# Sums of second-product weights by accumulating transfers instead of VectorE, in a Winograd feed-forward of one transformer layer

## The chip, the cores and the metric

The kernel runs on one core of a Trainium2 chip. The metric is the device time of one execution in microseconds (us); a kernel's time is the median of its runs. Engines are named as in the profile: PE is TensorE (matmul), PEld its weight load, DVE is VectorE, ACT is ScalarE, POOL is GpSimd, SP is SyncE, whose queue starts most transfers.

## The reference

One layer of a diffusion transformer over 1024 tokens of width 1024, with 256 context tokens: a half-step SwiGLU feed-forward, token mixing (a grid Fourier transform beside a bidirectional chunkwise mLSTM), a second half-step feed-forward. All in f32. What the change touches is the second product of the two feed-forwards of the 1024 tokens, `(silu(a) * b) @ w2`, with w2 of 2816 x 1024:

```python
def swiglu(u, w13, w2):
    a, b = jnp.split(u @ w13, 2, axis=-1)
    return (jax.nn.silu(a) * b) @ w2

def half_ffn(h, shift, scale, gate, g_pre, g_post, w13, w2):
    u = modulate(rmsnorm(h, g_pre), shift, scale)
    return h + 0.5 * gate * rmsnorm(swiglu(u, w13, w2), g_post)
```

The adaLN values (shift, scale, gate) are products of a conditioning vector with `w_ada`, nine chunks of 1024.

## The kernel before, in words

Every matmul runs in three passes on operands split into a high and a low part (`mm3`: hi·hi, hi·lo, lo·hi). A split is a cast on ACT and a subtraction on VectorE: L145 and L146 in `split_act`, L140 and L141 in `wunit`.

The feed-forwards use a Winograd scheme: the product of 2 x 2 blocks in seven products instead of eight, for sums of the left blocks a and of the right blocks b. `ffn_in` forms the left operands and writes the seven of them to a DRAM scratch `gx` (`put`, L479; the sums are made in `sink`, with `add` and `sub` of L582 and L583). `wino_out`, called once for each feed-forward, does the seven products with w2, one after another in the order 1, 6, 7, 4, 5, 3, 2. The blocks of w2 are b11, b12 (upper rows, left and right half of the columns) and b21, b22. The right operands are b11 for product 1; T2 = b22 − b12 + b11 for 6; T3 = b22 − b12 for 7; b21 − T2 for 4; b12 − b11 for 5; b22 for 3; b21 for 2. Each product has 11 pieces k of 128 rows, taken in six steps of two (the last has one); a piece takes 12 matmuls of 128x512, a product some 30 us.

For each step, `weights(n, s)` makes the right operand and splits it to `wh` and `wl` (three buffers each), and `operand` (L774) loads a left operand X from `gx` to a tile `t` and splits it to two tiles `g`. Weights come in two ways, both by SP: `raw` (L733) loads 512 KB, two pieces, to a tile `wr` (three buffers); `held` (L738) loads 256 KB to a tile `g`, of which there are 36, shared with the split X. T2 and T3 stay in `g` from product 1 or 6 to product 4 or 7. The sums of weights are `tt`, L727, on VectorE:

```python
            elif n == 6:
                b12 = raw(0, s, 1)
                for c, k in zip(cs, s):
                    T3[k] = held(1, k, 1)
                    tt(T3[k], T3[k], b12[:, c], SUB)
                    tt(T2[k], T3[k], T2[k], ADD)
```

Beside the products runs background work, issued in portions between matmuls (`tick`): in the first run of `wino_out` the remaining adaLN chunks (`ada_rest`: loads of `w_ada` at L247, sums at L253 on VectorE, small matmuls L263) and the preparation of the context; in the second the transposition of the residual stream to tokens (`to_tokens`: load `u<-h` L1556, transposes L1560, stores to `h2t` L1563). A scheduler orders the instructions of every engine ahead of time; the queue of each engine is in order, and tiles come from pools whose buffers are reused when their readers are done. `post` (L293 on) makes the gains with which a block's output is scaled.

Of the kernel before, what the change touches and what calls it, by code (L numbers as in the profile page):

```python
# [13 lines left out]
ALU = mybir.AluOpType  # L14
# [3 lines left out]
ND = D // P  # L18
SEQ = 1024
CTX = 256  # L20
TB = 512
# [13 lines left out]
class Kernel:  # L35
# [259 lines left out]
    def post(self, s, i):  # L295

        nc = self.nc
        t = self.const([P, ND], f"post{s}{i}")
        nc.vector.scalar_tensor_tensor(
            t, self.ada[s][:, (3 * i + 2) * 8 : (3 * i + 3) * 8], 1.0 if i == 1 else 0.5,  # L300
            self.norm_g[:, (2 * i + 1) * 8 : (2 * i + 2) * 8], op0=ALU.mult, op1=ALU.mult)
        return t


# [127 lines left out]
    NP = NF // 2  # L432
# [101 lines left out]
    def pair_products(self, q, n0, W, U, gx, gates):  # L534


        nc = self.nc
        p, h = q // 2, q % 2

        def product(n, acc=None):  # L540
            wh, wl = W[n]
            new = acc is None
            if new:
                acc = self.mm()
            for k in range(4):
                self.tick(1 / 8)
                c = slice(k * P, (k + 1) * P)
                self.mm3(acc, (wh[:, c], wl[:, c]), (U[n][0][k], U[n][1][k]), new and k == 0, k == 3, not new)
            return acc

        made = {}

        def sink(t, j, b):
            if h == 0:
                gates[j, b] = self.s512("m")
                nc.scalar.activation(gates[j, b], t, AF.Silu)
                return
            made[j, b] = self.gated(t, gates.pop((j, b)))
            if (j, b) != (0, 1):
                self.put(p, made[j, b], gx, {(0, 0): 1, (1, 0): 2, (1, 1): 4}[j, b])  # L560
            else:

                a11, a21, a22 = made[0, 0], made[0, 1], made[1, 1]
                s1, s2 = self.s512("t"), self.s512("t")
                add(s1, a21, a22)
                self.put(p, s1, gx, 5)
                sub(s2, s1, a11)
                self.put(p, s2, gx, 6)
                sub(a21, a11, a21)
                self.put(p, a21, gx, 7)  # L570
                made["s2"] = s2
            if (j, b) == (1, 0):
                s4 = self.s512("t")
                sub(s4, made[1, 0], made["s2"])
                self.put(p, s4, gx, 3)

        def copy(src):
            t = self.s512("t")
            nc.scalar.copy(t, src)
            return t  # L580

        add = lambda o, x, y: nc.vector.tensor_tensor(o, x, y, op=ALU.add)  # L582
        sub = lambda o, x, y: nc.vector.tensor_tensor(o, x, y, op=ALU.subtract)  # L583
        if p >= n0:
            A = product(1)
            p1 = copy(A)
            yield 1
            E = product(2)
            add(p1, E, p1)
            sink(p1, 0, 0)  # L590
            yield 2
            product(6, A)
            u2 = copy(A)
            yield 6
            Dp = product(7)
            p7 = copy(Dp)
            yield 7
            product(5, A)
            y = copy(A)
            add(p7, p7, y)  # L600
            sink(p7, 1, 1)
            yield 5
            product(4, Dp)
            add(u2, Dp, u2)
            sink(u2, 0, 1)
            yield 4
            product(3, A)
            sink(A, 1, 0)
            yield 3
            return  # L610
        p1 = W["p1"]
        if h == 1:
            made[0, 0] = self.s512("t")
            nc.sync.dma_start(made[0, 0], gx[0, p * P : (p + 1) * P, :])
        u2 = self.s512("t")
        add(u2, product(6), p1)
        yield 6
        Dp = product(7)
        p7 = copy(Dp)
        add(p7, p7, u2)  # L620
        yield 7
        C = product(5)
        add(p7, C, p7)
        sink(p7, 1, 1)
        yield 5
        product(4, Dp)
        t = self.s512("t")
        add(t, Dp, u2)
        sink(t, 0, 1)
        yield 4  # L630
        product(3, C)
        add(u2, C, u2)
        sink(u2, 1, 0)
        yield 3
# [81 lines left out]

    def wino_out(self, w2, gx, tokens, done):


        nc = self.nc
        w = w2.rearrange("(p j c) o -> c j p o", j=2, c=P)
        NP = self.NP
        steps = [tuple(range(k, min(k + 2, NP))) for k in range(0, NP, 2)]
        T2, T3 = [None] * NP, [None] * NP
        tt = lambda o, x, y, op: nc.vector.tensor_tensor(o, x, y, op=op)  # L727
        ADD, SUB = ALU.add, ALU.subtract

        def raw(j, s, h):  # L730
            t = self.sb.tile([P, 1024], F32, tag="wr", bufs=3, name=self.name("wr"))
            v = t.rearrange("p (a b) -> p a b", a=2)
            nc.sync.dma_start(v[:, : len(s), :], w[:, j, s[0] : s[-1] + 1, h * TB : (h + 1) * TB])  # L733
            return t

        def held(j, k, h):
            t = self.s512("g")
            nc.sync.dma_start(t, w[:, j, k, h * TB : (h + 1) * TB])  # L738
            return t

        def weights(n, s):
            hi = self.sb.tile([P, 1024], F32R, tag="wh", bufs=3, name=self.name("wh"))
            lo = self.sb.tile([P, 1024], F32R, tag="wl", bufs=3, name=self.name("wl"))
            cs = [slice(i * TB, (i + 1) * TB) for i in range(len(s))]
            full = slice(0, len(s) * TB)
            one = None
            if n == 1:
                for k in s:
                    T2[k] = held(0, k, 0)
            elif n == 6:  # L750
                b12 = raw(0, s, 1)
                for c, k in zip(cs, s):
                    T3[k] = held(1, k, 1)
                    tt(T3[k], T3[k], b12[:, c], SUB)
                    tt(T2[k], T3[k], T2[k], ADD)
            elif n == 4:
                one = raw(1, s, 0)
                for c, k in zip(cs, s):
                    tt(one[:, c], one[:, c], T2[k], SUB)
            elif n == 5:  # L760
                one, b11 = raw(0, s, 1), raw(0, s, 0)
                tt(one[:, full], one[:, full], b11[:, full], SUB)
            elif n in (2, 3):
                one = raw(1, s, n - 2)
            if one is not None:
                self.split_act(hi[:, full], lo[:, full], one[:, full])
            else:
                for c, k in zip(cs, s):
                    self.split_act(hi[:, c], lo[:, c], (T3 if n == 7 else T2)[k])
            return [(hi[:, c], lo[:, c]) for c in cs]  # L770

        def operand(n, k):
# [12 lines left out]
        for n in (1, 6, 7, 4, 5, 3, 2):  # L785
# [4 lines left out]
            for s in steps:  # L790
                T = weights(n, s)
                X = [operand(n, k) for k in s]
                todo += [(k, x, t) for k, x, t in zip(s, X, T)]
                if n == 2 and s[-1] in steps[-2]:
                    continue
                order = [(i, d) for i in range(len(todo)) for d in range(4)]
                if n == 2 and len(todo) > 2:
                    order = [(i, d) for d in range(4) for i in range(len(todo))]
                for i, d in order:
                    k, x, t = todo[i]  # L800
                    self.tick(1 / 8)
                    c = slice(d * P, (d + 1) * P)
                    st, mv = (x, t) if tokens else (t, x)
                    self.mm3(acc[d], (st[0][:, c], st[1][:, c]), mv, new and k == 0, k == NP - 1, not new)
                    if n == 2 and k == NP - 1:
                        done(0, 0, d, kept[1][d], acc[d])
                todo = []
# [1002 lines left out]
```

## Time and profile before

| | us |
|---|---|
| median of 3 runs (2751.29 to 2759.47) | 2755.34 |
| profiled execution | 2761.97 |
| its span | 2760.1 |
| product 1, 6, 7, 4, 5 of the first run: from | 490, 524, 565, 599, 632 (5 ends at 672) |
| product 1, 6, 7, 4, 5 of the second run: from | 2516, 2558, 2594, 2624, 2656 (5 ends at 2688) |

The profile shows one execution. The granted TensorE clock over all of it was 0.986 of full speed. The starts of the products are read from the order of TensorE's matmuls on a time line. Rows of groups read: line, engine, operation, out<-in by the program's names, sizes, how many, then busy us in sum, mean ns of one, then the engine's idle time just before them and what ended most of it.

### The profile page before, as it was taken

To read this page: it belongs to the slowest core of one execution; us is meant where nothing else is said; L and a number is where in the kernel's file an instruction comes from. 1 tells how busy PE (TensorE), PEld (TensorE's weight loads), DVE (VectorE), ACT (ScalarE), POOL (GpSimd) and SP (SyncE) were. 2 spreads that over 40 slices of the span, in tenths; PEclk is the share of its full clock that TensorE was granted. 3 is DMA by queue.
4 is the path that set the end of the run, shared out by engine and by line. 5 is a ranking of instruction groups with operands and counts; after the bars stand their busy time and mean duration, and the time that the engine had idled before them with its cause. 6 is when DMAs were issued, how large, how long until landed. Compare 5 with 4: busy or idle time off the path is not lost.

```text
span 2760.1 us, 33923 instructions
## 1 busy us (share of the span) xinstructions
PE 2661.3 (96%) x11657; PEld 2114.7 (77%) x11657; DVE 1857.2 (67%) x3341; ACT 1106.8 (40%) x1893; POOL 100.6 (4%) x217
## 2 busy tenths in 40 slices
PE   8899999998999999999999999999999999998998
PEld 5688888776877777777777778778887788887776
DVE  5688887899786438565363674555667887863765
ACT  4543332444454337233333333433345433333552
POOL 1100000000000001000000000000001000000000
PEclk9999999999999999999999999999999999999999
DMA  9765454857686545325223452356556654536874
GB/s 300 242 206 164 155 167 133 309 190 252 210 252 211 170 134 173 102 69 155 79 77 103 133 142 77 94 150 196 181 157 210 183 169 153 168 107 198 293 247 139
DMA packets 426012, 472.51 MB, mean 171 GB/s; under 512 B 25497, under 2 KB 264642, under 8 KB 425840
## 3 DMA queue, kind: packets, MB, share of 16 engines
q1 hardware_dynamic: 424448, 468.53, 54.2%
q0 software_dynamic: 1248, 1.75, 0.2%
q8 instruction: 92, 1.51, 0.2%
q14 instruction: 80, 0.66, 0.1%
q10 hardware_dynamic: 144, 0.07, 0.0%
HBM read 373.21 MB, written 97.04 MB: 170 GB/s over the span
## 4 chain that ended last, share of the span: by engine, by line
PE 75%; DVE 9%; DMA 8%; issue 4%; ACT 2%; SPq 1%; POOL 0%; DVEq 0%; POOLq 0%; ACTq 0%
PE mm L153 67%; DMA m<-r_l 2%; PE aux L1147 2%; PE qc L1332 1%; DVE u L253 1%; DVE wl L141 1%; DVE g L146 1%; DMA ld<-in_w_ada_dram 1%; DMA ld<-h 1%; DMA u<-h 1%; DMA ld<-hn 1%; PE mm L234 1%; DMA t<-gx 0%; ACT wh L140 0%; DVE wl L146 0%
## 5 line engine op out<-in xcount | busy, mean ns | idle before, releaser
L153 PE MATMUL mm<-g,wh 128*128 128x512 f32 (+1 forms) x2552 | 839.6, 409 | 11.9 <-ACT g L145 5.0
L153 PEld LDWEIGHTS mm<-g,wh 128*128 128x128 f32 (+1 forms) x2552 | 484.2, 192 | 122.2 <-ACT wh L145 6.0
L153 PE MATMUL mm<-g,wl 128*128 128x512 f32 (+1 forms) x1276 | 510.7, 402 | 3.4 <-DVE wl L146 3.3
L153 PE MATMUL mm<-g,o 128*128 128x512 f32 x2112 | 497.7, 394 | 0.0
L153 PEld LDWEIGHTS mm<-g,o 128*128 128x128 f32 x2112 | 396.9, 188 | 93.7
L141 DVE TENSOR_TENSOR wl<-wr,wh 128x1024 fp32r<-128x1024 f32 x226 | 278.8, 1234 | 223.9 <-ACT wh L140 223.2
L140 ACT CAST wh<-wr 128x1024 fp32r<-128x1024 f32 x226 | 236.3, 1046 | 352.5 <-PE mm L153 307.3
L153 PE MATMUL mm<-wh,g 128*128 128x512 f32 x1032 | 331.2, 399 | 6.6 <-ACT g L145 3.9
L153 PEld LDWEIGHTS mm<-g,wl 128*128 128x128 f32 (+1 forms) x1276 | 243.8, 191 | 59.0 <-DVE wl L146 5.6
L153 PE MATMUL mm<-u,wh 128*128 128x512 f32 (+1 forms) x848 | 268.4, 398 | 7.5 <-DVE m L704 4.9
L153 PEld LDWEIGHTS mm<-wh,g 128*128 128x128 f32 x1032 | 194.1, 188 | 54.5 <-ACT g L145 4.1
L153 PE MATMUL mm<-wl,g 128*128 128x512 f32 x516 | 205.1, 397 | 0.0
L153 PEld LDWEIGHTS mm<-u,wh 128*128 128x128 f32 (+1 forms) x848 | 159.8, 190 | 46.0 <-DVE m L704 5.4
L153 PE MATMUL mm<-wh,u 128*128 128x512 f32 x544 | 176.4, 399 | 0.0
L153 PE MATMUL mm<-u,wl 128*128 128x512 f32 (+1 forms) x424 | 167.3, 397 | 2.3 <-DVE wl L141 2.3
L582 DVE TENSOR_TENSOR t<-mm,t 128x512 f32<-128x512 f32 x128 | 88.1, 688 | 78.8 <-PE mm L153 78.6
L146 DVE TENSOR_TENSOR g<-t,g 128x512 fp32r<-128x512 f32 x154 | 103.0, 687 | 38.9 <-ACT g L145 32.1
L153 PEld LDWEIGHTS mm<-wh,u 128*128 128x128 f32 x544 | 102.0, 188 | 22.5
L145 ACT CAST o<-wa 128x512 fp32r<-128x512 f32 x88 | 54.6, 622 | 156.0 <-PE mm L153 144.8
L145 ACT CAST wh<-wr 128x1024 fp32r<-128x1024 f32 (+1 forms) x72 | 62.5, 870 | 131.9 <-PE mm L153 55.2
L153 PEld LDWEIGHTS mm<-wl,g 128*128 128x128 f32 x516 | 97.2, 188 | 23.0 <-issue 0.7
L153 PE MATMUL mm<-wl,u 128*128 128x512 f32 x272 | 108.8, 400 | 2.1 <-DVE wl L141 2.1
(469 smaller groups left out, 3432.8 us busy)
## 6 DMA issues: line engine op xcount, KB each, us to landing
wr<-in_w_a_dram SPq DMA_DIRECT2D x124, 512.0 KB, 4.4
t<-gx SPq DMA_DIRECT2D x174, 256.0 KB, 4.0
wr<-in_w_in_dram SPq DMA_DIRECT2D x80, 512.0 KB, 3.8
wr<-in_w_b_dram SPq DMA_DIRECT2D x70, 512.0 KB, 4.5
gx<-m SPq DMA_DIRECT2D x88, 256.0 KB, 4.2
gx<-t SPq DMA_DIRECT2D x66, 256.0 KB, 4.3
ld<-in_w_ada_dram SPq DMA_DIRECT2D x64, 256.0 KB, 2.8
ld<-h SPq DMA_DIRECT2D x48, 256.0 KB, 3.8
```

Of the source, the lines that this page charges most:

```text
L140: nc.scalar.copy(hv, rv)
L141: nc.vector.tensor_tensor(lv, rv, hv.bitcast(F32), op=ALU.subtract)
L145: self.nc.scalar.copy(hi, src)
L146: self.nc.vector.tensor_tensor(lo, src, hi.bitcast(F32), op=ALU.subtract)
L153: mul = lambda x, y, start, stop: self.nc.tensor.matmul(out, x, y, start=start, stop=stop, skip_group_check=grown)
L234: nc.tensor.matmul(pt[:2, :], self.sc[:, k, :], t, start=k == 0, stop=k == ND - 1)
L253: nc.vector.scalar_tensor_tensor(acc[s], t, self.sc[:, k, s : s + 1], acc[s], op0=ALU.mult, op1=ALU.add)
L582: add = lambda o, x, y: nc.vector.tensor_tensor(o, x, y, op=ALU.add)
L1147: nc.tensor.matmul(pt[:, :257], kw[:, i * P : (i + 1) * P], vaug, start=True, stop=True)
L1332: nc.tensor.matmul(pt[:, :257], at(q, i, c), C[:, i * 257 : (i + 1) * 257], start=i == 0, stop=i == 1)
```

## The change

The sums of weights leave VectorE. `grow(t, x)` starts a transfer on POOL's queue that adds x to the tile t. In product 1, b11 is loaded to T6 and split; b22 is loaded to T7, b12 is added to it by a transfer from DRAM, and T7 is then added to T6 by a transfer between tiles. Product 6 uses T6, product 7 T7; product 4 adds T6 to a loaded b21, product 5 adds b12 from DRAM to a loaded b11, 512 KB at once. Per run that is 11 + 11 + 11 + 6 = 39 such transfers, 78 in all.

Since a transfer only adds, signs move: the left operands 5, 6 and 3 are made with other signs in `sink` (three of the sums there, two of them now of the form (−x) − y), and the right operands are T7 = b22 + b12, T6 = T7 + b11, b21 + T6 and b11 + b12. The right half of the output columns comes out negated, which one multiplication of the gains by −1 in `post` takes back. VectorE's row goes from 3178 instructions to 3102.

```diff
@@ post @@
+        if s == 0 and i != 1:
+            nc.vector.tensor_scalar_mul(t[:, ND // 2 :], t[:, ND // 2 :], -1.0)
@@ sink @@
-                add(s1, a21, a22)
+                sub(s1, a22, a21)
-                sub(s2, s1, a11)
+                neg(s2, s1, a11)
-                sub(s4, made[1, 0], made["s2"])
+                neg(s4, made["s2"], made[1, 0])
+        neg = lambda o, x, y: nc.vector.scalar_tensor_tensor(o, x, -1.0, y, op0=ALU.mult, op1=ALU.subtract)
@@ wino_out @@
-        tt = lambda o, x, y, op: nc.vector.tensor_tensor(o, x, y, op=op)
+        part = lambda j, s, h: w[:, j, s[0] : s[-1] + 1, h * TB : (h + 1) * TB]
+        two = lambda t, s: t.rearrange("p (a b) -> p a b", a=2)[:, : len(s), :]
+        grow = lambda t, x: nc.gpsimd.dma_start(t, x, accum_op=ALU.add)
@@ weights @@
             if n == 1:
                 for k in s:
-                    T2[k] = held(0, k, 0)
-            elif n == 6:
-                b12 = raw(0, s, 1)
-                for c, k in zip(cs, s):
-                    T3[k] = held(1, k, 1)
-                    tt(T3[k], T3[k], b12[:, c], SUB)
-                    tt(T2[k], T3[k], T2[k], ADD)
+                    T6[k] = held(0, k, 0)
             elif n == 4:
                 one = raw(1, s, 0)
                 for c, k in zip(cs, s):
-                    tt(one[:, c], one[:, c], T2[k], SUB)
+                    grow(one[:, c], T6[k])
             elif n == 5:
-                one, b11 = raw(0, s, 1), raw(0, s, 0)
-                tt(one[:, full], one[:, full], b11[:, full], SUB)
+                one = raw(0, s, 0)
+                grow(two(one, s), part(0, s, 1))
...
-                    self.split_act(hi[:, c], lo[:, c], (T3 if n == 7 else T2)[k])
+                    self.split_act(hi[:, c], lo[:, c], (T7 if n == 7 else T6)[k])
+            if n == 1:
+                for k in s:
+                    T7[k] = held(1, k, 1)
+                    grow(T7[k], w[:, 0, k, TB:])
+                    grow(T6[k], T7[k])
```

Three places of the order show it. First, SP's queue early in product 1 of the first run, before. A row has line, operation, out<-in with the numbers of the tiles, and size. `t` takes an X from `gx`, `g` a piece of w2 (here b11, for T2):

```order
L774 DMA t_964_4266<-gx_318 128x512
L774 DMA t_967_4272<-gx_318 128x512
L774 DMA t_974_4312<-gx_318 128x512
L738 DMA g_962_4258<-in_w2_a_dram 128x512
L738 DMA g_963_4260<-in_w2_a_dram 128x512
L774 DMA t_977_4318<-gx_318 128x512
L738 DMA g_972_4304<-in_w2_a_dram 128x512
L738 DMA g_973_4306<-in_w2_a_dram 128x512
```

And after (lines are shifted: X at L780, pieces of w2 at L745):

```order
L780 DMA t_968_4282<-gx_318 128x512
L780 DMA t_971_4288<-gx_318 128x512
L780 DMA t_980_4336<-gx_318 128x512
L745 DMA g_964_4266<-in_w2_a_dram 128x512
L745 DMA g_965_4268<-in_w2_a_dram 128x512
L745 DMA g_966_4274<-in_w2_a_dram 128x512
L745 DMA g_967_4278<-in_w2_a_dram 128x512
L780 DMA t_983_4342<-gx_318 128x512
```

Behind two pieces of b11 (`g_964`, `g_965`, for T6) now stand the two of b22 (`g_966`, `g_967`, for T7) that were loaded in product 6. Second, POOL's queue around the first run of `wino_out`, before, with what each row waits for. The first two rows belong to `ffn_in`'s operands, the last three are powers of 128x2 or 128x4 for norms, two of them of stages behind:

```order
L456 TENSOR_TENSOR wa_323_1268<-u_47_205,u_55_213 128x512 [waits DVE_49]
L455 TENSOR_TENSOR b_322_1267<-u_43_201,u_51_209 128x512 [waits DVE_49]
L311 TENSOR_TENSOR rx_c_4482<-rs_t_1018_4480,mhalf_73 128x2 [waits DVE_49]
L311 TENSOR_TENSOR rs_r_1417_6109<-rs_t_1416_6107,mhalf_73 128x4 [waits DVE_49]
L311 TENSOR_TENSOR r1_1_6438<-rs_t_1492_6436,mhalf_73 128x4 [waits DVE_49]
```

After, behind `rx_c` (DMASW are transfers that POOL started, DMAHW those of SP):

```order
L736 DMA g_954_4220<-in_w2_a_dram 128x512 [waits DMAHW5_49,DMASW4_49,PE_49]
L736 DMA g_955_4224<-in_w2_a_dram 128x512 [waits DMAHW4_49,DMAHW6_49,DMASW5_49,PE_49]
L736 DMA g_952_4212<-g_954_4220 128x512 [waits DMAHW2_49,DMASW6_49,DMAHW3_49,DMASW4_49,DVE_49]
L736 DMA g_953_4214<-g_955_4224 128x512 [waits DMASW7_49,DMAHW4_49,DMASW5_49,DVE_49]
L736 DMA wr_1199_5246<-g_952_4212 128x512 [waits DMAHW1_49,DMAHW2_49,DMAHW0_49,DMAHW7_49,DMASW6_49,DMASW0_49]
L736 DMA wr_1199_5246<-g_953_4214 128x512 [waits DMASW7_49,DMASW1_49]
L736 DMA g_966_4274<-in_w2_a_dram 128x512 [waits DMAHW5_49,DMASW2_49,PE_49]
L736 DMA g_967_4278<-in_w2_a_dram 128x512 [waits DMAHW6_49,DMASW3_49,PE_49]
L736 DMA g_964_4266<-g_966_4274 128x512 [waits DMAHW3_49,DMASW2_49,DVE_49]
L736 DMA g_965_4268<-g_967_4278 128x512 [waits DMAHW4_49,DMASW3_49,DVE_49]
```

The first step's T7 (`g_954`, `g_955`) takes b12, T6 (`g_952`, `g_953`) takes T7, and product 4's first raw (`wr_1199`) takes T6, ahead of the second step's T7: three transfers in a row that each wait for the one before. Third, VectorE in product 6, before. `g_962` and `g_963` are T2 of the second step, `g_1052` and `g_1053` its T3, `u` are the sums of adaLN:

```order
L727 TENSOR_TENSOR g_1052_4612<-g_1052_4612,wr_1051_4610 128x512
L727 TENSOR_TENSOR g_1053_4616<-g_1053_4616,wr_1051_4610 128x512
L727 TENSOR_TENSOR g_962_4258<-g_1052_4612,g_962_4258 128x512
L727 TENSOR_TENSOR g_963_4260<-g_1053_4616,g_963_4260 128x512
L146 TENSOR_TENSOR g_1056_4627<-t_1054_4624,g_1055_4626 128x512
L146 TENSOR_TENSOR wl_1050_4609<-g_962_4258,wh_1049_4608 128x512
L146 TENSOR_TENSOR wl_1050_4609<-g_963_4260,wh_1049_4608 128x512
```

After, the same step, where `g_964` and `g_965` are T6:

```order
L146 TENSOR_TENSOR wl_1058_4643<-g_964_4266,wh_1057_4642 128x512 [waits DMASW4_49,PE_49]
L146 TENSOR_TENSOR wl_1058_4643<-g_965_4268,wh_1057_4642 128x512 [waits DMASW5_49,Activation_49]
L146 TENSOR_TENSOR g_1061_4651<-t_1059_4648,g_1060_4650 128x512 [waits DMAHW7_49,Activation_49]
L253 SCALAR_TENSOR_TENSOR u_1029_4524<-u_1056_4634,sc_83,u_1029_4524 128x512 [waits DMAHW6_49,DVE_49]
L146 TENSOR_TENSOR g_1064_4657<-t_1062_4654,g_1063_4656 128x512 [waits DMAHW0_49,Activation_49]
```

The four sums are gone, and the first subtraction for the weights waits for transfers that POOL started (DMASW), with the splits of X and the sums of adaLN queued behind it.

More of the change, by code (lines that the diff above doesn't have):

```diff
@@ L725, in wino_out @@
         steps = [tuple(range(k, min(k + 2, NP))) for k in range(0, NP, 2)]
-        T2, T3 = [None] * NP, [None] * NP
-        tt = lambda o, x, y, op: nc.vector.tensor_tensor(o, x, y, op=op)
-        ADD, SUB = ALU.add, ALU.subtract
+        T6, T7 = [None] * NP, [None] * NP
+        part = lambda j, s, h: w[:, j, s[0] : s[-1] + 1, h * TB : (h + 1) * TB]
+        two = lambda t, s: t.rearrange("p (a b) -> p a b", a=2)[:, : len(s), :]
+        grow = lambda t, x: nc.gpsimd.dma_start(t, x, accum_op=ALU.add)
         def raw(j, s, h):
             t = self.sb.tile([P, 1024], F32, tag="wr", bufs=3, name=self.name("wr"))
-            v = t.rearrange("p (a b) -> p a b", a=2)
-            nc.sync.dma_start(v[:, : len(s), :], w[:, j, s[0] : s[-1] + 1, h * TB : (h + 1) * TB])
+            nc.sync.dma_start(two(t, s), part(j, s, h))
             return t
```

## The prediction

> **What bounds the kernel now.** The page comes first: what is busy, and how full the transfers are in 40 slices of 69 us.
>
> ```profile
> span 2760.1 us, 33923 instructions
> PE 2661.3 (96%) x11657; PEld 2114.7 (77%) x11657; DVE 1857.2 (67%) x3341; ACT 1106.8 (40%) x1893; POOL 100.6 (4%) x217
> DMA  9765454857686545325223452356556654536874
> PE 75%; DVE 9%; DMA 8%; issue 4%; ACT 2%; SPq 1%; POOL 0%; DVEq 0%; POOLq 0%; ACTq 0%
> ```
>
> TensorE is the bound, and the chain of work that ended last (the fourth line) runs through it for 75%. So a VectorE operation removed is worth only what TensorE waits for it. The transfers are near full in slice 8 (483 to 552 us) and high again around slice 37, where the two runs of `wino_out` begin. Next, therefore, the table of windows cut at the ends of the products (1 and 6; 7; 4; 5 of the first run, then the same of the second). Its columns are busy time of each engine, then granted clock, DMA share and GB/s.
>
> ```profile
> 470.00:486.00 16.00, 15.03 (x74) 12.22 (x72) 9.46 (x15) 4.51 (x8) 0.00 (x0) 1.00 0.30 106
> 486.00:524.00 38.00, 34.01 (x135) 27.45 (x136) 26.65 (x44) 16.36 (x29) 0.00 (x0) 0.91 0.91 329
> 524.00:565.00 41.00, 35.95 (x145) 27.13 (x144) 39.22 (x66) 16.84 (x31) 0.00 (x0) 0.92 0.73 250
> 486.00:565.00 79.00, 69.96 (x278) 54.58 (x279) 65.87 (x109) 33.20 (x59) 0.00 (x0) 0.91 0.82 288
> 565.00:599.00 34.00, 33.52 (x149) 25.88 (x148) 31.62 (x54) 17.94 (x32) 0.00 (x0) 1.00 0.61 201
> 599.00:632.00 33.00, 31.91 (x141) 24.63 (x139) 31.56 (x57) 16.74 (x30) 0.00 (x0) 1.00 0.67 210
> 632.00:672.00 40.00, 32.58 (x123) 23.70 (x124) 35.95 (x51) 14.30 (x22) 0.00 (x0) 0.91 0.85 271
> 2497.00:2513.00 16.00, 15.63 (x78) 12.86 (x76) 8.42 (x13) 4.26 (x8) 0.00 (x0) 1.00 0.34 122
> 2513.00:2594.00 81.00, 72.51 (x327) 56.02 (x328) 46.93 (x74) 42.47 (x76) 0.00 (x0) 0.98 0.93 299
> 2594.00:2624.00 30.00, 30.00 (x130) 24.15 (x130) 22.17 (x35) 17.88 (x33) 0.00 (x0) 1.00 0.76 255
> 2624.00:2656.00 32.00, 32.00 (x139) 25.79 (x138) 22.12 (x29) 16.41 (x29) 0.00 (x0) 1.00 0.73 241
> 2656.00:2688.00 32.00, 32.00 (x139) 25.77 (x138) 22.04 (x32) 17.27 (x30) 0.56 (x1) 1.00 0.79 263
> ```
>
> Two limits stand here. In products 6 and 5 of the first run VectorE is busy 39.22 of 41 and 35.95 of 40 us, and TensorE idles 5.0 and 7.4. In product 1 of the first run, and in products 1 and 6 of the second, it is the transfers: 0.91 and 0.93, with VectorE at 0.58 over the second (46.93 of 81). Who ended the idle time is in the groups of TensorE: 486 to 565 (first three rows), 632 to 672 (two), 2513 to 2594 (two).
>
> ```profile
> L153 PE MATMUL mm<-g,wh 128*128 128x512 f32 x178 | 58.4, 418 | 5.0 <-ACT g L145 5.0
> L153 PE MATMUL mm<-g,wl 128*128 128x512 f32 x89 | 35.6, 415 | 1.5 <-DVE wl L146 1.5
> L263 PE MATMUL aux<-u,sel 128*2 128x512 f32 x7 | 2.7, 455 | 3.5 <-DVE u L146 2.0 <-ACT u L145 1.5
> L153 PE MATMUL mm<-g,wh 128*128 128x512 f32 x77 | 25.9, 433 | 5.9 <-ACT wh L145 4.0 <-DVE g L146 2.0
> L153 PE MATMUL mm<-g,wl 128*128 128x512 f32 x38 | 14.9, 422 | 2.0 <-DVE wl L146 1.8
> L153 PE MATMUL mm<-wh,g 128*128 128x512 f32 x178 | 58.1, 404 | 3.9 <-ACT g L145 3.9
> L1560 PE MATMUL qc<-ident,u 128*128 128x128 f32 x60 | 9.8, 288 | 5.0 <-DMA u<-h 3.9 <-ACT g L145 1.1
> ```
>
> The waits of product 6 (1.5 + 3.5) and product 5 (5.9 + 2.0) are VectorE's backlog; the single 5.0 and 3.9 at each run's start wait for a split of X, that is for its load. A stall costs more than itself: the granted clock halves afterwards.
>
> ```profile
> 557.70:564.50 6.80, 5.97 (x15) 4.41 (x16) 5.59 (x10) 3.84 (x7) 0.00 (x0) 0.50 0.66 212
> 643.00:646.40 3.40, 3.33 (x9) 1.82 (x7) 3.40 (x6) 1.26 (x3) 0.00 (x0) 0.51 0.97 334
> 667.00:670.30 3.30, 3.30 (x8) 2.65 (x9) 2.44 (x4) 0.70 (x2) 0.00 (x0) 0.50 0.84 290
> ```
>
> At half clock 6.8 us do the work of 3.4. So VectorE's backlog costs 5.0 + 3.4 = 8.4 us in product 6 and 7.4 + 1.7 + 1.7 = 10.8 in product 5. That is the most the change can win, 19.2 us, all in the first run: in products 7 to 5 of the second TensorE has no idle time.
>
> **What the change removes.** In each run, 22 sums for product 6, 11 for product 4, 6 double ones for product 5:
>
> ```profile
> L727 DVE TENSOR_TENSOR g<-g,wr 128x512 f32<-128x512 f32 x22 | 14.9, 687 | 10.9 <-DMA g<-in_w_b_dram 10.9
> L727 DVE TENSOR_TENSOR g<-g,g 128x512 f32<-128x512 f32 x22 | 14.8, 685 | 0.1
> L727 DVE TENSOR_TENSOR wr<-wr,g 128x512 f32<-128x512 f32 x22 | 14.7, 686 | 1.6 <-DMA wr<-in_w_b_dram 1.6
> L727 DVE TENSOR_TENSOR wr<-wr,wr 128x1024 f32<-128x1024 f32 (+1 forms) x12 | 13.6, 1132 | 1.8 <-DMA wr<-in_w_b_dram 1.8
> L253 DVE SCALAR_TENSOR_TENSOR u<-u,sc,u 128x512 f32<-128x512 f32 x56 | 37.9, 745 | 0.3 <-DMA u<-in_w_ada_dram 0.3
> L583 DVE TENSOR_TENSOR t<-t,t 128x512 f32<-128x512 f32 x20 | 13.8, 692 | 0.7
> ```
>
> Per run that is (14.9 + 14.8 + 14.7 + 13.6)/2 = 29.0 us of VectorE: 14.9 in product 6, more than its 8.4 of stalls and lost clock, and 6.8 in product 5, at most the 10.8. The new signs cost nothing: some 40 sums go from 692 ns (L583) to the form of L253 at 745, about 2 us under TensorE while VectorE has slack (9.46 of 16 us busy in 470:486), and two operations of 128x4.
>
> **What it adds: 78 accumulating transfers.** No row shows one; the bounds come from plain copies. Over 486:524 the 16 DMA engines gave 0.91 x 38 = 34.6 us to 329 GB/s x 38 us = 12.5 MB, that is 47.7 pieces of 256 KB: 0.725 us of all engines each. Low end: a sum costs a copy, 0.725 (it cannot move less). High end: it reads two operands and writes one, two copies, 1.45. I take 1.45, since both operands must be read; both ends stay in the range. The Trainium skill ("Collectives: The Full Stack", Part 3, "The bandwidth ceiling: the fold count and why AG ≠ RS ≠ AR") says that an add in the transfer engines reads two sources on one ring, and gives a measured ratio of 1.93 to a copy; by it a sum would be 1.40 and the total below some 2 us lower. No run here shows it yet.
>
> The sums of product 6 are now made in products 1 and 6, from loads that start in product 1. The loads that go, or move ahead of the stage:
>
> ```profile
> L733 SPq DMA_DIRECT2D wr<-in_w_a_dram x6: 333/384/384, 514.9 to 556.7; - x6
> ```
>
> Of these six, the first three hold the last five k of b12 (5 x 0.725 saved); the other three are product 4's first raws, 6 x 0.725, for which the three `wr` buffers are now free before product 1, where 470:486 has room (0.30). The loads of the first sums' own operand move from product 6 into product 1, among X's on SyncE's queue: 11 issues of 0.33 to 0.38 us there, and no more bytes over the two products. So products 1 and 6 gain 22 x 1.45 − 11 x 0.725 = 31.9 − 8.0 = 23.9 us of transfers.
>
> First run: 0.82 x 79 = 64.8, and 88.7 with the sums, in a stage of 79: **+9.7**, the transfers being its bound; the 8.4 that VectorE gives up lies under that. Second: 0.93 x 81 = 75.3, + 23.9, less three tiles of token transposes, load and store, that slide past product 6 in the order of SyncE (3 x 2 x 0.725 = 4.4) = 94.9 in 81: **+13.9**. Products 7 and 4 take product 4's sums: 20.7 + 8.7 of 34 and 22.1 + 7.3 of 33 in the first; 22.8 + 8.7 of 30 (1.5 over, left in the range) and 23.4 + 7.3 of 32 in the second: 0. Product 5: one raw becomes a sum, + 11 x 0.725 = 8.0, and half the `wr` buffers free let product 3's raws slide by some 4.4: 34.0 + 8.0 − 4.4 = 37.6 of 40, **−2.4** in the first run; 25.3 + 3.6 of 32, 0 in the second. There a sum also stands in each buffer's cycle, ahead of ACT's cast and whatever ACT has queued behind it:
>
> ```profile
> L141 DVE TENSOR_TENSOR wl<-wr,wh 128x1024 fp32r<-128x1024 f32 x226 | 278.8, 1234 | 223.9 <-ACT wh L140 223.2
> L140 ACT CAST wh<-wr 128x1024 fp32r<-128x1024 f32 x226 | 236.3, 1046 | 352.5 <-PE mm L153 307.3
> wr<-in_w_a_dram SPq DMA_DIRECT2D x124, 512.0 KB, 4.4
> rb<-in_b_in_dram POOLq DMA_DIRECT2D x4, 256.0 KB, 3.9
> L1000 POOL DMA_DIRECT2D rb<-in_b_in_dram x4 | 2.3, 573 | 37.8 <-ACT u L408 29.6 <-PE aux L263 7.5 <-DVE o L1011 0.7
> ```
>
> Load 4.4, issue 0.6, sum 3.9 (a plain transfer of POOL's) to twice that, cast 1.05 and subtraction 1.23 are 11.2 to 15.1 us, with three buffers 3.7 to 5.0 a step, and a step is 32/6 = 5.3: hidden.
>
> Sum: +9.7 + 13.9 − 2.4 = +21.2 on the profiled execution (2762.0, 6.6 above the median of the runs). On the median, 2755.3 + 21.2 = 2776.5: **2776 us**. A difference below 0.3% (8.3 us) can't be told from none.
>
> A rule that speaks against the change stands by the rows 0.91 and 0.93: the Trainium skill ("DMA: Bandwidth & Descriptors", "Issuing engines are not separate DMA queues") says that transfers begun by GpSimd run on the same 16 engines and interleave with SyncE's. So by it POOL's idleness buys no bandwidth; the sum above adds the shares, and were POOL's transfers on engines of their own it would be case B. No row here tests it.
>
> **The rivals.** B, faster: a sum costs a copy, and it fits. Then products 1 and 6 of the first run hold 64.8 + 8.0 = 72.8 us of transfers, against 79 − 8.4 = 70.6 for TensorE: −6.2. Product 5 has 29.6 of transfers and loses its 10.8. Second: 75.3 + 8.0 − 4.4 = 78.9 of 81: 0. Together −17.0: 2738. For it: VectorE at 39.22 of 41. Against it: two operands.
>
> C, slower still: the chain on POOL. Its queue is in order, and each step's second sum waits for the first to land, product 4's for the second, ahead of the next step's. I count 9 landings in a row and 28 issues up to product 6's last operand: 9 x 3.9 + 28 x 0.573 = 51 us, against about 64 from the first loads (487) to that operand's use (551). It decides from a landing of 5.3; at two copies, 7.8, it is 86, 22 late in each run: 2755 + 2 x 22 = 2800. Behind the wait stand VectorE's L146 for the weights and, in its queue, the splits of X and the sums of L253.
>
> D, no change: elastic transfers. Ahead of the stages 0.30 and 0.34 of 16 us are used; 10 us of room each to a share of 0.95. If the added loads and sums run early there, 9.7 and 13.9 shrink to 0 and 3.9, with −2.4: 2757. Against it: the second operand of the pair is split in product 1 before it may grow.
>
> **How the numbers follow.** A 0.45 (2776), C 0.17 (2800), B 0.20 (2738), D 0.18 (2757). So faster by over 0.3% 0.20, within 0.18, slower 0.62. The range 2740 to 2820 leaves out about half of B below, and above C a landing of more than 9 us.
>
> **What would show it.** In the profile after: no L727 on VectorE, and waits L146 in products 6 and 5 gone (right for B and A alike); the DMA share of products 1 and 6 at 0.95 or above in both runs, with TensorE waiting for X (ACT g L145) more than 5.0 and 3.9: A. TensorE waiting for `wl`/`wh` split from `g` in product 6, released by POOL's transfers, with shares below 0.9: C. The price itself: busy time of the software queue over 78 sums. The forecast is wrong if a sum takes one copy's time, or if the stalls at 490 and 2516 stay as they are.

## The result, and the profile after

The changed kernel takes 2807.6 us (median of 4 runs, 2801.1 to 2815.1) against 2757.4 for the kernel before beside it (2751.3 to 2765.6): a ratio of 1.0179, 95% interval 1.0161 to 1.0196, slower by 50 us. The forecast was +21. The direction was right and the time lies inside the range, but the size was short by more than half.

The page of the changed kernel, the lines that answer to those of before, and the row of the queue that holds the sums (packets, MB, share of the 16 engines):

```profile
span 2806.4 us, 34039 instructions
PE 2672.4 (95%) x11657; PEld 2124.0 (76%) x11657; DVE 1808.0 (64%) x3265; ACT 1107.4 (39%) x1893; POOL 172.3 (6%) x295
DMA  9774546968686545325233442456546554429794
q0 software_dynamic: 13760, 24.83, 5.0%
PE 72%; DMA 11%; DVE 8%; issue 5%; ACT 2%; SPq 1%; POOL 1%; DVEq 0%; POOLq 0%; ACTq 0%
```

VectorE lost 49 us of work and TensorE gained 11 us of busy time for the same 11657 matmuls: it ran at a lower clock, 0.978 over the whole execution against 0.986. In the chain that ended last, DMA rose from 8% to 11%.

Where the time went is read by cutting both traces at the ends of the products: from the end of the last matmul of `ffn_in` to the end of the last copy (or last addition) of each product's results. These ends come some us later than the cuts by TensorE's own matmuls in the prediction.

| us, one profiled execution | 1 | 6 | 7 | 4 | 5 | 3 | 2 |
|---|---|---|---|---|---|---|---|
| before, first run | 39.1 | 41.1 | 33.6 | 33.3 | 47.0 | 35.4 | 30.5 |
| after, first run | 51.1 | 44.4 | 33.5 | 42.1 | 45.9 | 31.4 | 31.1 |
| before, second run | 46.3 | 35.3 | 30.8 | 31.8 | 35.3 | 29.6 | 28.7 |
| after, second run | 76.2 | 34.3 | 30.9 | 34.5 | 35.2 | 29.6 | 28.7 |

First products 1 and 6 of the second run in the kernel before, each by itself (columns as before: us, busy time of PE, PEld, DVE, ACT, POOL, then granted clock, DMA share, GB/s):

```profile
2513.00:2559.00 46.00, 38.53 (x172) 29.39 (x172) 20.89 (x33) 22.55 (x41) 0.00 (x0) 0.96 0.91 288
2559.00:2594.00 35.00, 33.98 (x156) 26.62 (x156) 26.03 (x42) 19.92 (x36) 0.00 (x0) 1.00 0.95 315
```

Then the changed kernel: the 16 us ahead of the first run, its products 1, 6, both together, and 4; the 16 us ahead of the second run, its products 1, 6, both together, and 7:

```profile
467.00:483.00 16.00, 16.00 (x78) 13.04 (x76) 9.13 (x14) 3.72 (x7) 4.49 (x5) 1.00 0.68 157
483.00:534.00 51.00, 37.53 (x139) 28.95 (x139) 22.62 (x36) 17.61 (x32) 13.39 (x16) 0.83 1.08 314
534.00:578.50 44.50, 35.50 (x141) 26.55 (x140) 32.86 (x55) 18.60 (x36) 7.04 (x8) 0.92 0.87 246
483.00:578.50 95.50, 73.03 (x279) 55.50 (x279) 55.49 (x90) 36.21 (x67) 20.43 (x23) 0.87 0.98 282
612.00:654.00 42.00, 35.60 (x147) 26.83 (x146) 31.21 (x53) 20.69 (x37) 8.06 (x8) 0.93 0.93 254
2512.00:2528.00 16.00, 15.58 (x78) 12.82 (x76) 8.35 (x13) 4.34 (x8) 4.42 (x5) 1.00 0.71 179
2528.00:2604.00 76.00, 51.99 (x182) 39.08 (x183) 15.72 (x24) 22.42 (x41) 19.08 (x22) 0.75 1.04 281
2604.00:2638.00 34.00, 32.22 (x147) 25.74 (x146) 20.71 (x32) 21.80 (x40) 0.86 (x1) 1.00 0.89 285
2528.00:2638.00 110.00, 84.20 (x327) 64.82 (x328) 36.43 (x56) 44.23 (x80) 19.93 (x23) 0.83 1.00 282
2638.00:2669.00 31.00, 31.00 (x134) 24.98 (x133) 17.49 (x25) 17.09 (x31) 1.72 (x2) 1.00 0.50 146
```

Product 1 is the place: a DMA share of 1.08 and 1.04, a clock of 0.83 and 0.75. (Recorded packet times can add up to a little over 1, and not only where two queues run: 1.06 at 500 to 510 us of the kernel before, where all of it was SyncE's. Such a share is read as full.) In the second run it alone takes 29.9 of the 46 us. VectorE is busy 15.7 of 76 us there: it has been relieved where it never was the bound. The waits of TensorE in products 1 and 6 of the second run (engine, line, what ended them: us, times, longest):

```profile
PE qc L1566 <- DMA u<-h: 16.0, 7, 4.7
PE mm L153 <- ACT g L145: 9.3, 3, 8.2
```

Both are loads that came late: the residual stream for the transposes (3.9 us of waiting before) and X.

### The profile page after: what moved, and what is told of

Same layout as the page of the kernel before. It is cut to its first block, busy times and chain, and to the rows that moved or that the text cites. A ratio compares the mean times of both kernels' runs of the same rounds, so it can differ in the third digit from the quotient of the medians.

```text
span 2806.4 us, 34039 instructions
## 1 busy us (share of the span) xinstructions
PE 2672.4 (95%) x11657; PEld 2124.0 (76%) x11657; DVE 1808.0 (64%) x3265; ACT 1107.4 (39%) x1893; POOL 172.3 (6%) x295
## 3 DMA queue, kind: packets, MB, share of 16 engines
q0 software_dynamic: 13760, 24.83, 5.0%
## 4 chain that ended last, share of the span: by engine, by line
PE 72%; DMA 11%; DVE 8%; issue 5%; ACT 2%; SPq 1%; POOL 1%; DVEq 0%; POOLq 0%; ACTq 0%
PE mm L153 64%; DMA m<-r_l 2%; PE aux L1153 2%; DMA u<-h 1%; PE qc L1338 1%; DVE wl L141 1%; DMA t<-gx 1%; DMA ld<-in_w_ada_dram 1%; DMA ld<-h 1%; DMA wa<-in_w_ada_dram 1%; DMA wr<-in_w_b_dram 1%; DMA ld<-xT_c 1%; DMA g<-in_w_a_dram 1%; DVE g L146 1%; ACT wh L140 1%
## 5 line engine op out<-in xcount | busy, mean ns | idle before, releaser
L153 PE MATMUL mm<-wh,g 128*128 128x512 f32 x1032 | 339.9, 407 | 15.0 <-ACT g L145 9.3
L145 ACT CAST g<-t 128x512 fp32r<-128x512 f32 x154 | 90.5, 618 | 76.9 <-DMA t<-gx 42.8
L145 ACT CAST wh<-wr 128x1024 fp32r<-128x1024 f32 (+1 forms) x72 | 62.7, 870 | 146.3 <-PE mm L153 59.7
L145 ACT CAST o<-wa 128x512 fp32r<-128x512 f32 x88 | 54.6, 622 | 157.0 <-PE mm L153 150.8
```

Source lines behind the costliest of these rows:

```text
L145: self.nc.scalar.copy(hi, src)
L153: mul = lambda x, y, start, stop: self.nc.tensor.matmul(out, x, y, start=start, stop=stop, skip_group_check=grown)
```

## The experiments

The theory behind the forecast is called the bandwidth theory: a sum takes the 16 DMA engines as long as two copies, and the loads that TensorE needs stand in line with it. Its main rival is the chain theory: each sum waits on GpSimd's in-order queue for one before it. A ratio is to the kernel before, run beside it.

**The signs alone.** The new signs, all 39 sums a run additions on VectorE, in the places of its sums and differences before:

```diff
+            elif n == 6:
+                b12 = raw(0, s, 1)
+                for c, k in zip(cs, s):
+                    T7[k] = held(1, k, 1)
+                    tt(T7[k], T7[k], b12[:, c])
+                    tt(T6[k], T6[k], T7[k])
...
-                    grow(one[:, c], T6[k])
+                    tt(one[:, c], one[:, c], T6[k])
```

> The new signs alone: every sum of weights is an addition on VectorE, in the places where the kernel before has its subtractions; no transfer is begun by GpSimd. All theories expect the time of before, 2757 us within 0.3%: some 40 sums that take 50 ns more under TensorE. A time above 2765 would put part of the 50 us on the signs.

Measured 2754.4 us, ratio 0.9999 (0.9985 to 1.0014). The signs cost nothing, so the kernels below that use them compare with before directly.

**No sums at all.** Part of the computation is missing here:

```diff
-        grow = lambda t, x: nc.gpsimd.dma_start(t, x, accum_op=ALU.add)
+        grow = lambda t, x: None
```

> The changed kernel with the 78 accumulating transfers left out (products 6, 7, 4 and 5 use the bare blocks, so part of the computation is missing), all loads in their new places. Bandwidth theory (a sum takes 1.5 us of all 16 engines, and the loads that TensorE needs in product 1 wait): faster than before by VectorE's relief, 2738 to 2745. Order theory (the loads of b22 moved into product 1 hold up X): still slower than before, 2775 or more, with product 1 of the second run over 60 us.

Measured 2740.2 us, ratio 0.9953 (0.9936 to 0.9971). Product 6 of the first run falls from 41.1 to 32.4 (8.4 forecast for VectorE's backlog), 5 from 47.0 to 37.8, 3 from 35.4 to 31.4. Product 1 of the second run rises from 46.3 to 53.1: that is the part of the order theory, the loads of b22. So VectorE's relief is real, 13 us net, and the transfers cost 2807.6 − 2740.2 = 67 us on top of it (63 when each time is set against the kernel before that ran beside it). The first run alone gives back 22 us, more than the 19.2 that the prediction named as the most, since product 3 gains 4 too; here, though, the loads of b12 are missing as well.

**Copies in place of sums.** Same queue, same waits, no addition (the sums are missing):

```diff
-        grow = lambda t, x: nc.gpsimd.dma_start(t, x, accum_op=ALU.add)
+        grow = lambda t, x: nc.gpsimd.dma_start(t, x)
```

> The changed kernel with plain copies in place of the 78 accumulating transfers (same queue, same waits; the sums are missing, a copy overwrites). Bandwidth theory: the software queue's share falls from 1.5 to some 0.75 us a piece of 256 KB, the second run's products 1 and 6 hold 74 + 24 x 0.75 = 92 us of transfers instead of 110, so 2775 to 2785. Chain theory (each sum waits on GpSimd's queue for one before it, and what counts is the landing): landings stay at 5 to 7 us, and the time stays at 2800 or more.

Measured 2773.6 us, ratio 1.0073 (1.0046 to 1.0099). Copies bring about half of the cost: none 2740, copies +33, sums +63 to 67. That is just under the bandwidth theory's range and far from the chain theory's 2800. The order and the waits are the same in the last two, but a chain of copies is also a little quicker: in product 1 of the second run they land in 5.1 to 5.7 us, the sums in 5.7 to 7.3. So this run alone does not settle it.

**Product 6's sums one product later.**

```diff
-            if n == 1:
-                for k in s:
-                    T7[k] = held(1, k, 1)
-                    grow(T7[k], w[:, 0, k, TB:])
-                    grow(T6[k], T7[k])
+            elif n == 6:
+                for k in s:
+                    T7[k] = held(1, k, 1)
+                    grow(T7[k], w[:, 0, k, TB:])
+                    grow(T6[k], T7[k])
```

> The changed kernel with the sums of product 6 (and the loads of b22) issued with product 6's steps instead of product 1's. Bandwidth theory: product 1 goes back to within 3 us of before (39 and 46 us), the same excess appears in product 6, in sum 2790 to 2810. Chain theory: two landings now stand right ahead of each step's use, product 6 grows by 20 us or more in each run, and the time is above 2820.

Measured 2828.9 us, ratio 1.0278 (1.0252 to 1.0304): the chain theory's figure, and above the bandwidth theory's range. Product 6 takes 61.7 and 64.4 us. In product 6 of the first run ACT's cast waits for the sum between tiles:

```profile
ACT wh L145 <- DMA g<-g: 32.3, 9, 11.1
```

Product 1 does not go all the way back (46.1 and 53.7 us): the scheduler begins the sums there as soon as their tiles allow. So the chain can cost, when the sums stand right ahead of their use. Whether it does in the changed kernel, the next ones ask.

**The sums of products 6 and 7 alone, and of b12 alone.** The first has products 4 and 5 add on VectorE (44 transfers left); the second also T6 + T7, in product 6, so that 22 transfers are left and none waits for another:

```diff
             if n == 1:
                 for k in s:
                     T7[k] = held(1, k, 1)
                     grow(T7[k], w[:, 0, k, TB:])
-                    grow(T6[k], T7[k])
```

> Only the sums for products 6 and 7 are accumulating transfers (44), products 4 and 5 add on VectorE. Bandwidth theory for products 1 and 6, queue theory for product 4 (ACT's cast waits for product 5's first sum): products 1 and 6 keep most of their growth (first run 95.5 to some 90, second 110.5 to some 103, since product 4's sums no longer run there early), product 4 goes back to 33, in sum 2785 to 2795. Rival (the sums of products 4 and 5 are half of the loss): 2775 or less.

> A quarter of the sums: only b12 is added by accumulating transfers (22 in all, in place of the loads of b12), in product 1; T6 + T7 and products 4 and 5 add on VectorE, T6 + T7 in product 6. Bandwidth theory: 11 x (1.47 - 0.73) = 8 us more of transfers in products 1 and 6 of each run: the second run's go from 81.6 to 88 to 91, the first run's stay within 3 of 80, in all 2760 to 2768. Chain theory (what costs is sums that wait for sums on GpSimd's queue; here none does): no growth, 2745 to 2755.

Measured 2790.8 us, ratio 1.0132 (1.0115 to 1.0150), and 2771.0 us, 1.0060 (1.0042 to 1.0077). The first is as forecast, and rules its rival out. The second decides against the chain as the main cause: without any sum that waits for a sum, product 1 of the second run takes 66.6 us. It is also 3 us above the bandwidth range, as products 1 and 6 of the second run take 66.6 + 32.1 = 98.7 us where 88 to 91 were forecast, and that miss shows what was wrong in my way of counting. Here are the transfers of product 1 of the second run alone, in six kernels. Before:

```profile
q1 hardware_dynamic: 11168, 13.34, 90.6%
t<-gx SPq DMA_DIRECT2D x17, 256.0 KB, 4.4
g<-in_w_b_dram SPq DMA_DIRECT2D x13, 256.0 KB, 4.4
```

No sums:

```profile
q1 hardware_dynamic: 12846, 15.37, 90.1%
```

Copies in place of sums:

```profile
q1 hardware_dynamic: 12702, 15.44, 73.8%
q0 software_dynamic: 1620, 5.31, 22.3%
```

The sums of b12 alone:

```profile
q1 hardware_dynamic: 12859, 15.74, 72.5%
q0 software_dynamic: 1296, 2.36, 20.3%
```

The sums of products 6 and 7 alone:

```profile
q1 hardware_dynamic: 12820, 15.66, 64.9%
q0 software_dynamic: 2193, 4.00, 30.9%
```

The changed kernel:

```profile
q1 hardware_dynamic: 12693, 15.44, 60.9%
q0 software_dynamic: 3249, 5.91, 43.4%
t<-gx SPq DMA_DIRECT2D x17, 256.0 KB, 6.0
g<-in_w_b_dram SPq DMA_DIRECT2D x18, 256.0 KB, 6.4
```

Share times length gives the us of all 16 engines, and MB over 0.262 the pieces of 256 KB:

| second run, product 1 | length | SyncE's transfers | GpSimd's | sum | us a piece of GpSimd's |
|---|---|---|---|---|---|
| before | 46.3 | 41.9 | | 41.9 | |
| no sums | 53.1 | 47.8 | | 47.8 | |
| copies | 63.0 | 46.5 | 14.0 | 60.5 | 0.69 |
| b12 alone | 66.6 | 48.3 | 13.5 | 61.8 | 1.50 |
| products 6, 7 alone | 73.0 | 47.4 | 22.6 | 70.0 | 1.48 |
| all sums | 76.2 | 46.4 | 33.1 | 79.5 | 1.47 |

The length follows the sum of transfers, line by line. Against the kernel without sums, the 13.5 us of the sums of b12, which wait for no sum, lengthen product 1 by 13.5 us. With the chain, 22.6 us of sums lengthen it by 19.9, 33.1 by 23.1, and 14.0 of copies by 9.9: a us of transfers costs less there, not more, so the chain adds nothing that shows. SyncE's transfers grow by some eight pieces, mostly five loads of b22 and three of the tokens' transfers, and stay at that; GpSimd's come on top; each piece takes SyncE 0.82 us before and 0.79 after (41.9 and 46.4 over 13.34 and 15.44 MB), so no transfer of SyncE's got dearer. A sum also moves in nearly twice as many packets as a copy, beside taking twice the time: over the whole kernel GpSimd's queue has 13760 packets with the sums and 8128 with the copies, for the same bytes, and 1248 without either.

**Product 5's sums alone,** products 6, 7 and 4 adding on VectorE as in the first experiment (what is left of the transfers):

```diff
             elif n == 5:
                 one = raw(0, s, 0)
                 grow(two(one, s), part(0, s, 1))
```

> Only product 5's sums are accumulating transfers (12 of 512 KB at most), the others additions on VectorE. Bandwidth theory: products 5 and 3 of the first run give back 5 us (82.4 to some 77, as in the changed kernel), nothing in the second, where the transfers of product 5 have room: 2748 to 2753. Chain theory (ACT's cast of product 5's first weights waits for its sum, and the copies of product 4's results queue behind it): product 4 of the first run grows from 33 to 38 us, and the sum is nought: 2755 to 2760.

Measured 2762.6 us, ratio 1.0023 (1.0010 to 1.0037), above both forecasts. Product 4 of the first run, in which no sum is a transfer any more, takes 42.5 us (33.3 before, 42.1 in the changed kernel, 33.2 with the sums of 6 and 7 alone): product 5's sums cost 9 us ahead of their product. The waits of ACT and of TensorE from product 4 into 5 (598 to 660 us):

```profile
ACT wh L145 <- DMA wr<-in_w_a_dram: 22.2, 5, 7.2
PE mm L153 <- ACT st L789: 5.2, 1, 5.2
PE aux L263 <- ACT u L145: 4.0, 1, 4.0
```

And the longest of these waits with what stands next in ACT's queue (start, us):

```profile
636.61 1.04 ACT L145 CAST wh<-wr 128x1024 fp32r<-128x1024 f32 x1 [7.18 <-DMA wr<-in_w_a_dram]
637.57 1.55 ACT L789 COPY st<-mm 128x512 f32<-128x512 f32 x3
```

The casts of product 5's first weights wait five times, up to 7.2 us. The longest wait ends with a sum that GpSimd issued at 628.8 us and that landed at 636.5. Behind that cast in ACT's queue stand three of the four copies of product 4's results (`st`), and TensorE waits 5.2 us for them before it can reuse the accumulators. Products 5 and 3 give back only 2.9 us (82.4 to 79.5).

**Product 5's sums one product ahead,** in the first run alone, in the tiles that T7 leaves free (the other sums on VectorE, as in the first experiment):

```diff
+            if n == 4 and not tokens:
+                for k in s:
+                    T5[k] = held(0, k, 0)
+                    grow(T5[k], w[:, 0, k, TB:])
```

> Only product 5's sums of the first run are accumulating transfers, made one product ahead: b11 is loaded to the tiles that T7 leaves free, in product 4, and b12 is added there; all else on VectorE. Queue theory (what costs in products 4 and 5 is that a cast waits for its sum at once): product 4 stays at 33 to 36 instead of 42.5, products 5 and 3 fall from 82.4 to 70 to 74, so 2745 to 2750. Bandwidth theory (11 x 0.73 + 11 x 1.5 us more of transfers in product 4, whose share is 0.67): product 4 grows to 40 or more, the gain is lost, 2755 or more.

Measured 2755.4 us, ratio 0.9999 (0.9990 to 1.0007). The wait of ACT is gone and products 5 and 3 fall to 38.0 and 33.9, nearly as without sums, but product 4 still takes 42.4. Its window, and TensorE's longest wait:

```profile
599.00:632.00 33.00, 25.51 (x109) 19.42 (x109) 25.65 (x45) 12.72 (x25) 7.08 (x9) 0.92 0.92 263
PE mm L153 <- DVE g L146: 9.0, 3, 6.1
```

Now it is the split of X that comes late, at a share of 0.92 (0.67 before). So the 9 us are paid here too, by another wait, as the bandwidth theory had it.

**The token transposes begun after product 6** of the second run, in the changed kernel, in the kernel before, and together with the last experiment:

```diff
-        self.later(self.to_tokens(self.h2, 1, h2t), self.to_tokens(self.h2, 0, h2t), rate=1.0)
+        self.later(self.to_tokens(self.h2, 1, h2t), self.to_tokens(self.h2, 0, h2t), rate=1.3)
+        self.credit = -14.0
```

> The changed kernel with the 16 tiles of token transposes of the second run begun only after product 6, at a higher rate. Bandwidth theory: 16 x 2 x 0.73 = 23 us of transfers leave products 1 and 6 of the second run (110.5 us, of which the transfers fill all) for product 7, whose share is 0.50: those two products fall to 88 to 95, the kernel to 2785 to 2795. Chain theory: the sums' own waits stay, products 1 and 6 stay above 100 and the kernel at 2800 or more.

> The kernel before with the same edit alone. Bandwidth theory: products 1 and 6 of the second run (81.6 us at a share of 0.93) lose 23 us of transfers and the waits of the transposes, and get 7 to 12 us shorter; products 7 and 4 get the transposes (10 us of TensorE), so 2750 to 2755 in all. Chain theory says nothing of it.

> The last kernel and the token transposes begun after product 6 in the second run, together: the gains add if they are in different runs of the second products: 1 to 4 us below the last kernel.

Measured 2806.7 us, ratio 1.0190 (1.0168 to 1.0213); 2752.5, 0.9991 (0.9980 to 1.0002); 2752.0, 0.9984 (0.9974 to 0.9994). In the changed kernel products 1 and 6 fall to 48.7 + 36.8 = 85.5 us, even below the 88 to 95 of the bandwidth theory, and yet the time is that of the chain theory: products 7, 4 and 5 go from 100.6 to 122.3. Product 4 there, and the same product of the kernel before with the same edit:

```profile
2641.30:2688.50 47.20, 35.65 (x164) 27.58 (x163) 17.27 (x22) 20.09 (x36) 7.41 (x7) 1.00 1.01 285
```

```profile
2605.60:2642.80 37.20, 35.49 (x167) 27.95 (x166) 21.32 (x27) 19.89 (x36) 0.00 (x0) 1.00 0.94 305
```

Its sums and the moved tokens fill the engines again (1.01). In the kernel before the edit moves 13.9 us out of products 1 and 6, of which 12.6 come back in 7, 4 and 5. No version that computes all of it beats the kernel before by over 0.3%.

**GpSimd's own additions** in place of transfers, for b22 + b12 and products 4 and 5:

```diff
+        pt = lambda o, x, y: nc.gpsimd.tensor_tensor(o, x, y, op=ALU.add)
...
-                    grow(one[:, c], T6[k])
+                    pt(one[:, c], one[:, c], T6[k])
```

> Sums by GpSimd's own additions instead of transfers: b22 + b12 (11 a run), product 4's (11) and product 5's (6 of 128x1024); T6 + T7 stays on VectorE, all loads as in the kernel before. A 128x512 addition took GpSimd 2.19 us in the kernel before, so 24 us in product 6, 24 in 4 and 26 in 5, each within its product. Bandwidth theory: no transfer is added, VectorE's relief shows in part, 2742 to 2750. Rival (it is the wait on GpSimd's queue and its speed that cost): products 6 and 5 of the first run get longer than 41 and 47 us, 2757 or more.

Measured 2772.6 us, ratio 1.0064 (1.0040 to 1.0089). Products 1, 7 and 4 of the first run grow to 43.3, 41.4 and 41.7, though no transfer was added. The time is the rival's, but the products that the rival named got shorter: 6 takes 38.7 us and 5 takes 44.6. What changed for the worse is read in VectorE's rows, before and then with GpSimd adding, 485 to 700 us:

```profile
L146 DVE TENSOR_TENSOR wl<-g,wh 128x512 fp32r<-128x512 f32 x31 | 20.8, 686 | 8.9 <-ACT wh L145 8.9
L253 DVE SCALAR_TENSOR_TENSOR u<-wa,sc,u 128x512 f32<-128x512 f32 x28 | 19.5, 748 | 4.1 <-DMA wa<-in_w_ada_dram 4.1
```

```profile
L146 DVE TENSOR_TENSOR wl<-g,wh 128x512 fp32r<-128x512 f32 x31 | 26.2, 871 | 6.5 <-ACT wh L145 6.5
L253 DVE SCALAR_TENSOR_TENSOR u<-wa,sc,u 128x512 f32<-128x512 f32 x28 | 25.6, 953 | 1.1 <-DMA wa<-in_w_ada_dram 1.1
```

The same operations take 686 and 748 ns alone, 871 and 953 on average here. The time line shows where the average comes from: of the 31 operations of the first row, the 19 that met no addition of GpSimd took 682 ns, and the 11 that lay wholly within its additions took 1114 ns on average, up to 1786. ACT's casts also waited 11.7 us for GpSimd's sums (565 to 655 us), the kind of wait that my rival had named; how the 12 us of the first run divide between the two was not tested.

## Why the prediction was right or wrong

By its own steps, in the profiled executions:

| part | forecast | measured |
|---|---|---|
| first run, products 1 and 6 | +9.7 | 95.5 − 80.2 = +15.3 |
| first run, 7 and 4 | 0 | +8.7, all in 4 |
| first run, 5, 3 and 2 | −2.4 | −4.5 |
| second run, 1 and 6 | +13.9 | 110.5 − 81.6 = +28.9 |
| second run, the rest | 0 | +2.7 |
| elsewhere | 0 | −4.9 |

**The bound was right.** The transfers fill products 1 and 6 of both runs (shares of 0.98 and 1.00), and TensorE waits for the split of X (ACT g L145) 11.0 and 9.3 us there, 5.0 and 3.9 before: the signs that the prediction gave for its own case.

**The price of a sum** was right: 1.45 taken, 1.47 to 1.50 measured, and 0.69 for a copy (0.725 taken). The reason given for it, a second operand to read, is not shown by these runs: the sums' packets were also nearly twice as many. The Trainium skill ("Collectives: The Full Stack", Part 3, "The bandwidth ceiling: the fold count and why AG ≠ RS ≠ AR") reports a measured ratio of 1.93 between a collective that copies and one that adds, and puts it down to two reads. Here the ratio is 1.47 over 0.69 to 0.725, 2.0 to 2.1, so these runs agree with its size. The Trainium skill ("DMA: Bandwidth & Descriptors", "Issuing engines are not separate DMA queues") also says that transfers begun by GpSimd run on the same 16 engines as SyncE's. These runs agree: 46.4 us of SyncE's and 33.1 of GpSimd's fill the 76.2 us of product 1.

**The largest term failed: the transfers of products 1 and 6 of the second run,** 94.9 forecast. There were 109.8 in a window of 110.5 us. The two rows of that window, before (2512.6 to 2594.3) and after (2527.6 to 2638.1):

```profile
q1 hardware_dynamic: 19530, 24.45, 92.6%
```

```profile
q1 hardware_dynamic: 19665, 24.62, 66.7%
q0 software_dynamic: 3547, 6.45, 32.7%
```

SyncE's transfers went from 75.7 to 73.7 us; I had taken 12.4 off them, and this is most of the 14.9 us that were missing. The loads that left (b12, product 4's raws) were replaced by others that ran ahead into the window, four more loads of X among them (40 against 36); product 7, at 0.50, is the product that they left. No token tile slid out, although three stores stand behind more loads of X in SyncE's order. And GpSimd's sums took 36.1 us, not 31.9: 24.6 pieces of them ran in it, not 22, since product 4's first sums were not held back for product 7. Behind that lies the error that the table of six kernels shows: two products were taken as one store of bandwidth. What can be issued early runs in product 1, and TensorE waits there; product 6, which the loads that left were to relieve, takes some 32 us of TensorE's own in any case (32.2 without sums), and the room in product 7, where the share fell from 0.76 to 0.50, can't be lent back. Counted by product 1 alone, from the rows of before: 41.9 + 5 loads of b22 at 0.725 + 22 x 1.45 = 77.4 us, against a length of 76.2. That count was made after the result, and the records hold 79.5 us of transfers.

**The first run's products 1 and 6** missed by less, 95.5 us at a share of 0.98 where 88.7 were forecast. Here SyncE's loads did leave, from 65.4 us to 58.0; what was short is mostly the sums, 24 pieces and 35.3 us instead of 22 and 31.9.

**Product 4 at nought** failed too. I counted the buffers' cycle of product 5 (11.2 to 15.1 us over three buffers) and found it hidden; a steady cycle says nothing of the first step, whose cast stands in ACT's queue ahead of product 4's copies. In the kernel with product 5's sums alone they cost 9 us, and five of the six there landed 7.3 to 10.3 us after their issue, where 3.9 to 7.8 were taken. The relief in 5 and 3 was there (13.2 us in the kernel without sums), and most of it was given back: the changed kernel keeps 5.1, of which 4.0 in product 3, while the forecast had its 2.4 in product 5.

**The rivals.** B was wrong on the price of a sum; its gain was near what VectorE's relief alone brings (17 forecast, 13 in the kernel without sums). C's time, 2800, is the nearest to the result, and its condition came true: the sums' median landing in products 1 and 6 was 5.7 to 8.2 us, above the 5.3 from which it decides. But its sign did not come: TensorE waited for weights split from `g` 3.7 us in the first run and 0.9 in the second. Nor is the chain needed, as sums without one already cost 17 us in products 1 and 6 of the second run. It does rule when the sums are issued late. That the time lies within the range is luck: the upper end was there for C, and the case that the forecast rests on was short by 29 us. D, elastic transfers, held in part: 0.30 and 0.34 ahead of the runs became 0.68 and 0.71. What stays open is what the chain adds in the changed kernel beside the full transfers, and how the 9 us of product 4 divide between ACT's queue and the transfers, since the kernel that removed the one met the other.

## What to carry to other kernels

Moving an addition into a transfer trades 0.69 us of one engine for 1.47 us of all 16: look at the DMA share of the stage in which the transfer will run, which is the earliest that its waits allow, not the one that needs the result. Count each such stage by itself, and leave off no transfer unless the order and the buffers say where else it runs. And see what stands behind the first wait on each in-order queue, not only whether the steady cycle fits.

## What the runs showed of the hardware that was not expected

In the stretch where GpSimd added 128x512 tiles (1.7 to 2.1 us each), VectorE's operations took up to 27% longer on average (686 to 871 and 748 to 953 ns); those that lay within an addition took 1114 ns on average instead of 682. And the clock fell further than I had counted: in product 1 of the second run TensorE was granted 0.75 of its speed against 0.96, so that its 182 matmuls were busy 52.0 us where 172 had been busy 38.5.
